# Raw output weights in nine places over the turned cached keys, late stores on ScalarE's queue, and a tile of its own for the sample group's sums

## The chip, the cores and the metric

One core of a Trainium2 chip runs the whole program, one launch. The metric is the device time of that launch in microseconds, the median over the runs shown. A separate profiled execution of the same program gives the trace from which all rows below are taken.

The core has five engines with instruction streams of their own, which meet only at semaphores: TensorE (PE, with its weight loads listed as PEld), VectorE (DVE), ScalarE (ACT), GpSimd (POOL) and SyncE (SP), which here does little but issue DMAs. A DMA is an instruction in the stream of the engine that issues it: if the tile it reads is not ready, or the tile it writes not free, the engine waits there, and everything behind it in that stream waits too. SBUF is the on-chip memory; PSUM holds the sums of matmuls.

## The reference, cut to what matters

One decoder layer over a prompt group (1024 new tokens) and a sample group (8 sequences of 8 tokens with 4096 cached positions). Both go through the same weights:

```python
z = h @ w_in                                  # projections, split into q, k, v, gates ...
o_sb  = stick_breaking(q_a, ..., sb_k, sb_v)  # the sample group's runs over the paged cache cache_sb
o_nsa = nsa_attend(q_b, ...)                  # compressed + selected + window attention
u = concatenate([o_sb * silu(gate_a), o_nsa * silu(gate_b)])
h = x + u @ w_out
y = h + sigmoid(h @ w_ple_gate) * (p @ w_ple)
```

The last two lines, for nine tiles of tokens, are the part of the program that the change is about: `w_out` and `w_ple_gate` are 1024x1024, `w_ple` is 256x1024.

## The kernel before, in words

The program runs in stages: projections for both groups; compression of the cached keys; then, interleaved, the sample group's stick-breaking over the cache (`phase_b`) and the prompt's sparse attention (`nsa_unit` in stage d, one unit for each pair of heads and block `i` of 128 tokens); at last the output projection (`Phase3`). The code states the steps and gives them due times; a scheduling layer then fixes, before the program runs, the order of the instructions in each engine's stream. So a change of a buffer or of a queue can move instructions on all engines.

**The sample group's cache.** Blocks of `cache_sb` arrive by SP's queue in tiles `bkv` (512 KB a load); VectorE turns the keys into `bkT` (L1477); TensorE forms scores `bz` (L1386) and sums `bo` (L1402). `finish` (L1538 to L1545) copies a group's sums into a tile `bs` and stores them to the scratch `s_oa_s` in eight DMAs. It runs twice, `finish(0)` in the middle of the stage and `finish(1)` at its end.

**The prompt's sparse attention.** A unit ends with its sums in PSUM, which ScalarE copies into `u` (printed as line L1731); for the last pair of heads (`pair == 3`) each of the eight units stores its 128x128 block to the scratch `s_uT` by SP's queue (L1278).

**The output projection.** Matmuls run in pieces of fp32r: each weight and each input is split into a high part, which GpSimd rounds off (`woh`, `wgh`, `wph`, L1602; `uh`, L1667), and a low part, which VectorE forms as raw minus high (`wol`, `wgl`, `wpl`, L1603; `ul`, L1668). `weight` takes a weight matrix 128 rows by 512 columns at a time: a raw tile `wr` of 256 KB is loaded by SP's queue (L1601), split, and its place is free again when VectorE is done. `w_out` has 16 such tiles, `w_ple` 4, `w_ple_gate` 16. In the kernel before the raw tiles of `w_out` have two places, in the same pool as `woh`/`wol`; those of the other two weights have three (`nwb`). The pool of `w_out` lies over the end of the cache tiles `bkv`, so it can be filled only once the stick-breaking is nearly over.

`a(t)` forms `h = x + u @ w_out` for a tile `t`: it loads `u`, the gate `g` and `x`, multiplies (L1660 to L1662, with a tanh on ScalarE), splits, and makes 48 products of 128x512 for a prompt tile. The sample group (`t == 8`) needs 32, with high and low part of its 64 tokens side by side in one operand; `product` then adds the two halves, through a tile that it takes from the ring of `g` (one place). `b(t)` is the rest: 48 products with `w_ple_gate`, 12 with `w_ple`. The order is a(8), a(7), a(0), a(6), b(8), b(7), and so on; prompt tiles stand in the order 7, 0, 6, 1, 5, 2, 4, 3. `u`, `g`, `uh` and `ul` have one place each, so `uh` of the next tile can be written only when the products of the tile before have read it.

The figures of the string `P3A` set the number of PSUM sums, of places and the lag; the seventh, `nwr`, is the number of places for the raw tiles of `w_out`.

Of the kernel before, what the change touches and what calls it, by code (L numbers as in the profile page):

```python
# [5 lines left out]
F32 = mybir.dt.float32  # L6
# [14 lines left out]
def hbm(ap, off, dims):  # L21
    return bass.AP(tensor=ap.tensor, offset=ap.offset + off, ap=[list(d) for d in dims])
# [5 lines left out]

def diagonals(K, pool):

    t = pool.tile([128, 128], F32, name="jpf")
    K.nc.gpsimd.iota(t, pattern=[[1, 128]], base=0, channel_multiplier=-1, allow_small_or_imprecise_dtypes=True)
    return t


def make_consts(K, pool):
    nc = K.nc
    K.id = pool.tile([128, 128], F32, name="idf")
    with K.tc.tile_pool(name="cj", bufs=1, reuse_waits="tile") as tmp:
# [899 lines left out]
def phase_d(K, es, part):  # L939
    nc, A, T = K.nc, K.A, K.T  # L940
# [233 lines left out]
    def nsa_unit(pair, h, i, last):  # L1174

        def gen():
# [8 lines left out]
            for c0 in range(0, W, 512):  # L1185
                w = min(512, W - c0)
# [85 lines left out]
            o = slice(i * 128, i * 128 + 128)  # L1272
            if ("u", pair) not in state:
                state["u", pair] = mid.tile([128, 1024], F32, name="u", bufs=1)
            u = state["u", pair]
            K.evac(u[:, o], av[:, :128])
            if pair == 3:
                nc.sync.dma_start(hbm(T["uT"], (512 + pair * 128) * 1024 + i * 128, [[1024, 128], [1, 128]]), u[:, o])  # L1278
            elif last:
                nc.sync.dma_start(hbm(T["uT"], (512 + pair * 128) * 1024, [[1024, 128], [1, 1024]]), u)  # L1280
        return gen
# [4 lines left out]
    if part == "s":  # L1286
# [7 lines left out]
        for pair in range(4):  # L1294
            x = [sb_unit(pair, h, i, i == 3) for i in order for h in range(2)]
# [5 lines left out]
    for pair in range(4):  # L1301
        g = nsa_prep(pair)()
        for t in P["p%d" % pair if pair % 2 == 0 else "p"]:
            L.append((pair * 8 + t, g))
        for n, i in enumerate(order):
            for h in range(2):
                g = nsa_unit(pair, h, i, n == 7)()
# [6 lines left out]
def phase_b(K, es, psb):  # L1314
# [3 lines left out]
    nc, A, T = K.nc, K.A, K.T  # L1318
# [219 lines left out]
    def finish(g4):  # L1538
        assert summed.count(g4) == 128
        o = wk.tile([128, 4, 128], F32, name="bs", bufs=2)  # L1540
        for i in range(4):
            (V.tensor_copy if i % 2 else S_.copy)(o[i * 32:i * 32 + 16], out[g4][i * 32:i * 32 + 16])
        for i in range(4):
            for h2 in range(2):
                nc.sync.dma_start(hbm(T["oa_s"], g4 * 32 * 512 + (i * 2 + h2) * 64, [[512, 8], [8 * 512, 4], [1, 64]]), o[i * 32 + h2 * 8:i * 32 + h2 * 8 + 8, :, h2 * 64:h2 * 64 + 64])  # L1545

    once = lambda f, *x: (f(*x) for _ in range(1))
    P = K.bstep
    g = start()
    L = [(t, g) for t in P["n"]]  # L1550
    for b in range(8):
        g = begin(b)
        L += [(b * 4 + t, g) for t in P["b"]]
        for n in range(4):
            x = Step(b, 3 - n)
# [13 lines left out]
class Phase3:  # L1569
# [3 lines left out]
    def __init__(s, K, es):  # L1573
        s.K = K
        P = lambda n, b, **k: es.enter_context(K.tc.tile_pool(name=n, bufs=b, side="right", **k, reuse_waits="tile"))
        s.wa = P("3a", 1)
        s.ps = [(P("3aps", 1, space=PSUM), K.p3acc[0], 3 - K.p3acc[0])]
        s.h = {}
        s.WO = s.weight(s.wa, "wo", K.A["w_out"], 8, 1)

    def open_b(s, es):
        K = s.K
        P = lambda n, b, **k: es.enter_context(K.tc.tile_pool(name=n, bufs=b, **k, reuse_waits="tile"))
        s.wb = P("3b", 1)
        s.ps.append((P("3bps", 1, space=PSUM), K.p3acc[1], 5 - K.p3acc[1]))
        s.K.nwr = K.nwb
        s.WP = s.weight(s.wb, "wp", K.A["w_ple"], 2, K.wbw)
        s.WG = s.weight(s.wb, "wg", K.A["w_ple_gate"], 8, K.wbw)

    def acc(s):  # L1590
        p, n, _ = s.ps[-1]
        return p.tile([128, 512], F32, name="acc", bufs=n)

    def weight(s, pool, name, src, nk, w):
        nc = s.K.nc
        hi = [pool.tile([128, nk, 512], F32R, name=f"{name}h{n}") for n in range(2)]
        lo = [pool.tile([128, nk, 512], F32R, name=f"{name}l{n}") for n in range(2)]
        for n in range(2):
            for k0 in range(0, nk, w):
                raw = pool.tile([128, w, 512], F32, name="wr", bufs=s.K.nwr if w == 1 else 2)  # L1600
                nc.sync.dma_start(raw, hbm(src, k0 * 128 * 1024 + n * 512, [[1024, 128], [128 * 1024, w], [1, 512]]))  # L1601
                nc.gpsimd.tensor_scalar(hi[n][:, k0:k0 + w], raw, 1.0, 0.0, op0=OP.mult, op1=OP.add)  # L1602
                nc.vector.tensor_tensor(lo[n][:, k0:k0 + w], raw, hi[n][:, k0:k0 + w].bitcast(F32), op=OP.subtract)  # L1603
        return hi, lo

    def product(s, X, W, n, nk, S):

        nc = s.K.nc
        acc = s.acc()
        if not S:  # L1610
            terms = [(a[:, k], b[:, k]) for k in range(nk) for a, b in ((X[0], W[0][n]), (X[0], W[1][n]), (X[1], W[0][n]))]
        else:
            terms = [(X[0][:, k], b[:, k]) for k in range(nk) for b in (W[0][n], W[1][n])]
        for i, (a, b) in enumerate(terms):
            nc.tensor.matmul(acc, a, b, start=i == 0, stop=i == len(terms) - 1)  # L1615
        if not S:
            return acc
        z = s.wa.tile([128, 8, 128], F32, name="g", bufs=1).rearrange("p a b -> p (a b)")[:64, 0:512]
        nc.scalar.copy(z, acc[64:128])
        nc.vector.tensor_tensor(z, acc[:64], z, op=OP.add)  # L1620
        return z
# [133 lines left out]
    return phase_b(K, es, es.enter_context(K.tc.tile_pool(name="psb", bufs=1, space=PSUM, side="right", reuse_waits="tile")))  # L1755


P3A = [int(x) for x in "2,3,3,2,2,1,2,3,1".split(",")]


def stage_d(K, steps, esb):
# [131 lines left out]
```

## Time and profile before

| what | us |
|---|---|
| median of 3 runs | 1827.23 |
| lowest and highest run | 1824.98, 1827.26 |
| the profiled execution | 1825.76 |
| its span in the trace | 1824.0 |

The span runs from the first instruction to the last that the trace shows; the 1.76 us beside it lie around the program. Over the whole span TensorE's matmuls are busy 89% of the time, VectorE 68%, ScalarE 48% and GpSimd 32%. Such shares mix stages with different limits, so the page is only where to begin: the stretch between the attention and the output projection, some 60 us near the end, is read from the timelines, the waits and the chain. The granted clock is the one that the throttle allows TensorE; it shows 1.00 (2.4 GHz) or 0.50 (1.2 GHz), and in a stretch the mean of the two. The mean over the profiled run is 0.946.

### The profile page before, as it was taken

How to read it: one execution, taken by the hardware profiler on the slowest of the kernel's cores; microseconds unless marked ns; L12 is line 12 of the kernel's file. 1: busy time of each engine (PE TensorE's matmuls, PEld its weight loads, DVE VectorE, ACT ScalarE, POOL GpSimd, SP SyncE). 2: the span in 40 equal slices, each digit the busy share in tenths (PEclk: the TensorE clock that was granted, in tenths of full speed). 3: DMA queues.
4: the chain of work that ended last, by engine and by line, in shares of the span. 5: the costliest groups of instructions: out<-in, count | busy, mean ns of one | idle time of the engine just before them, and what ended most of it. 6: DMA issues, size and time to landing. Idle time of an engine off the chain costs nothing.

```text
span 1824.0 us, 41667 instructions
## 1 busy us (share of the span) xinstructions
PE 1618.3 (89%) x15742; PEld 1377.0 (75%) x15742; DVE 1243.9 (68%) x2918; ACT 876.1 (48%) x2200; POOL 591.2 (32%) x1028
## 2 busy tenths in 40 slices
PE   4899999999987799999999679899799798499998
PEld 4799888988865699889888556667567566278887
DVE  5334755876876668888888897877788876645322
ACT  3212645655656334444344367777677777102111
POOL 2123002121311255555553144445244445410000
PEclk9899999999997899999999589999899999699999
DMA  7234113132106365555554997776988782723210
GB/s 252 74 90 126 62 58 117 54 108 63 57 32 147 126 209 193 185 193 198 188 187 142 369 305 251 241 269 224 307 302 289 262 278 67 231 75 93 87 50 35
DMA packets 186899, 300.80 MB, mean 165 GB/s; under 512 B 30145, under 2 KB 100610, under 8 KB 178434
## 3 DMA queue, kind: packets, MB, share of 16 engines
q1 hardware_dynamic: 145786, 207.14, 35.1%
q0 software_dynamic: 9216, 67.11, 11.1%
q10 hardware_dynamic: 31696, 23.88, 4.1%
q8 instruction: 124, 2.03, 0.5%
q14 instruction: 77, 0.63, 0.1%
HBM read 271.81 MB, written 30.48 MB: 166 GB/s over the span
## 4 chain that ended last, share of the span: by engine, by line
PE 39%; DVE 15%; DMA 11%; ACT 6%; issue 4%; POOL 3%; SPq 1%; ACTq 0%; POOLq 0%; DVEq 0%
PE acc L1615 11%; PE H L500 6%; DMA bkv<-in_cache_sb 5%; PE pt L1270 2%; PE bo L1402 2%; DMA raw<-in_cache_nsa,cidx 2%; PE bz L1386 2%; DVE bkT L1477 2%; PE acc L270 2%; PE pt L1247 2%; PE sc L672 2%; ACT bAT L1528 2%; PE cav L814 2%; PE acc L268 1%; DVE bs L1396 1%
## 5 line engine op out<-in xcount | busy, mean ns | idle before, releaser
L270 PE MATMUL acc<-whi,hh 128*128 128x256 f32 (+1 forms) x704 | 204.0, 291 | 5.3 <-DVE og L1733 2.7
L270 PE MATMUL acc<-wlo,hh 128*128 128x256 f32 (+1 forms) x704 | 201.6, 287 | 0.0
L270 PE MATMUL acc<-whi,hl 128*128 128x256 f32 (+1 forms) x704 | 200.7, 290 | 0.0
L1477 DVE STREAM_TRANSPOSE bkT<-bkv 128x512 f32<-128x512 f32 x256 | 171.5, 693 | 41.5 <-DMA bkv<-in_cache_sb 30.6
L270 PEld LDWEIGHTS acc<-whi,hh 128*128 128x128 f32 x704 | 135.1, 192 | 8.1 <-POOL whi L123 3.1
L481 ACT CAST XH<-xt 128x512 fp32r<-128x512 f32 x128 | 79.1, 618 | 122.5 <-PE H L500 112.4
L270 PEld LDWEIGHTS acc<-wlo,hh 128*128 128x128 f32 x704 | 135.1, 192 | 0.2 <-issue 0.2
L270 PEld LDWEIGHTS acc<-whi,hl 128*128 128x128 f32 x704 | 133.3, 192 | 0.7 <-issue 0.3
L1238 POOL TENSOR_SCALAR t<-t,nst 128x640 f32<-128x640 f32 (+7 forms) x128 | 93.4, 731 | 112.0 <-DVE nst L1229 48.4
L123 POOL TENSOR_SCALAR whi<-wraw 128x512 fp32r<-128x512 f32 (+1 forms) x60 | 53.3, 915 | 216.4 <-PE acc L245 153.2
L1247 PE MATMUL pt<-idf,t 128*128 128x128 f32 x528 | 91.7, 291 | 14.1 <-ACT aT L1731 7.0
L1402 PE MATMUL bo<-bkv,bAT 128*16 128x128 f32 x2048 | 84.8, 281 | 19.4 <-POOL bAT L1530 12.2
L651 POOL DMA_INDIRECT raw<-in_cache_nsa,cidx x64 | 66.9, 1046 | 102.5 <-DVE xt L476 53.7
L1386 PE MATMUL bz<-bkT,bQ 128*32 128x128 f32 x2048 | 92.7, 304 | 5.2 <-DVE ba L1506 3.3
L1530 POOL TENSOR_SCALAR bAT<-baT 32x128 f32<-32x128 f32 x256 | 77.6, 303 | 57.8 <-DVE baT L1520 36.8
L1731 ACT COPY aT<-pt 128x512 f32<-128x512 f32 (+3 forms) x167 | 76.9, 475 | 38.0 <-PE pt L1041 20.7
L500 PE MATMUL H<-w1hk,XH 128*128 128x256 f32 (+1 forms) x272 | 86.4, 318 | 9.8 <-ACT XH L481 8.2
L476 DVE STREAM_TRANSPOSE xt<-raw 128x512 f32<-128x512 f32 x132 | 88.0, 679 | 3.1 <-DMA raw<-in_cache_nsa,cidx 1.7
L1247 PEld LDWEIGHTS pt<-idf,t 128*128 128x128 f32 x528 | 59.7, 145 | 39.0 <-issue 13.5
L1085 DVE TENSOR_TENSOR_SCAN t<-ones,t 128x1024 f32<-128x1024 f32 (+7 forms) x64 | 87.0, 1360 | 0.7
L1402 PEld LDWEIGHTS bo<-bkv,bAT 128*16 128x16 f32 x2048 | 58.7, 99 | 36.7 <-POOL bAT L1530 22.3
L486 POOL TENSOR_TENSOR XL<-xt,XH 128x512 fp32r<-128x512 f32 x56 | 72.2, 1289 | 37.8 <-ACT XH L481 37.5
(464 smaller groups left out, 5040.9 us busy)
## 6 DMA issues: line engine op xcount, KB each, us to landing
bkv<-in_cache_sb SPq DMA_DIRECT2D x256, 512.0 KB
wraw<-in_w_in SPq DMA_DIRECT2D x28, 512.0 KB
x<-in_x_prompt SPq DMA_DIRECT2D x8, 512.0 KB
out_sb_rows_prompt<-o ACTq DMA_DIRECT2D x32, 128.0 KB
s_gT<-og ACTq DMA_DIRECT2D x16, 256.0 KB
cwin<-in_state_win SPq DMA_DIRECT2D x8, 512.0 KB
wr<-in_w_out SPq DMA_DIRECT2D x16, 256.0 KB
u<-s_uT SPq DMA_DIRECT2D x8, 512.0 KB
```

The costliest lines, as they stand in the source:

```text
L270: nc.tensor.matmul(acc[:, :w], a[:, k, t * 128:(t + 1) * 128], b[:, k, :w], start=i == 0, stop=i == 23)
L476: V.transpose(xt[:, :, e, :, b], raw[:, :, 0:256].rearrange("p l (k e c) -> p e l k c", e=2, c=32)[:, e])
L481: S_.copy(XH.rearrange("p a b -> p (a b)"), x.rearrange("p e k b s -> p (e k b s)"))
L500: nc.tensor.matmul(H[:m, kv * 256:kv * 256 + 256], x[:, c], y[:, l * 2 + e], start=start and l + kv + e + i == 0, stop=stop and l == 7 and ...
L1085: nc.vector.tensor_tensor_scan(a[:, ::-1], K.ones.to_broadcast([128, W]), a[:, ::-1], 0.0, op0=OP.mult, op1=OP.add)
L1238: nc.gpsimd.tensor_scalar(x, x, c, 1.0, op0=OP.mult, op1=OP.mult)
L1247: nc.tensor.transpose(pt[:, b * 128:(b + 1) * 128], x, K.id)
L1386: nc.tensor.matmul(z(h, g), q(j), kT(j), start=jj == 0, stop=jj == 1, skip_group_check=True, tile_position=(0, h * 32))
L1402: nc.tensor.matmul(oav[i * 32:i * 32 + 16], lhs(g, hp), v[:, i * 128:i * 128 + 128], start=first, stop=last, skip_group_check=True, tile_p ...
L1477: V.transpose(t.kT[f][:, :, i % 4], t.k[i].rearrange("p (j c) -> p j c", j=16))
L1530: G.tensor_scalar(o, i, 1.0, 0.0, op0=OP.mult, op1=OP.add)
L1615: nc.tensor.matmul(acc, a, b, start=i == 0, stop=i == len(terms) - 1)
```

## The change

Three things. First, the raw tiles of `w_out` get a pool of their own, `3r`, with nine places of 2 KB a partition instead of two. It is closed when the weights of `b` are opened. It lies over the place of `bkT`, the turned keys; its first place also overlaps the place of `bs` in `finish(1)`, the second the first bytes of `bkv`, and the other seven overlap only `bkT`. `woh` and `wol` move up by 2 KB a partition and lie over `bkv` as before. The raw tiles of `w_ple` and `w_ple_gate` keep three places. Second, the eight stores of `u` at L1278 and the eight stores of `finish(1)` at L1545 are issued by ScalarE instead of SyncE. Third, the sum of the sample group's two halves gets its own tile `z`, and no longer takes the one place of `g`.

```diff
             if pair == 3:
-                nc.sync.dma_start(hbm(T["uT"], ...), u[:, o])
+                nc.scalar.dma_start(hbm(T["uT"], ...), u[:, o])
...
-                nc.sync.dma_start(hbm(T["oa_s"], ...), o[...])
+                (nc.sync, nc.scalar)[g4].dma_start(hbm(T["oa_s"], ...), o[...])
...
-        s.WO = s.weight(s.wa, "wo", K.A["w_out"], 8, 1)
+        s.raws = ExitStack()
+        s.WO = s.weight(s.wa, "wo", K.A["w_out"], 8, 1, s.raws.enter_context(K.tc.tile_pool(name="3r", bufs=1, side="right", reuse_waits="tile")))
     def open_b(s, es):
         K = s.K
+        s.raws.close()
...
-        s.WP = s.weight(s.wb, "wp", K.A["w_ple"], 2, K.wbw)
-        s.WG = s.weight(s.wb, "wg", K.A["w_ple_gate"], 8, K.wbw)
+        s.WP = s.weight(s.wb, "wp", K.A["w_ple"], 2, K.wbw, s.wb)
+        s.WG = s.weight(s.wb, "wg", K.A["w_ple_gate"], 8, K.wbw, s.wb)
...
-                raw = pool.tile([128, w, 512], F32, name="wr", bufs=s.K.nwr if w == 1 else 2)
+                raw = raws.tile([128, w, 512], F32, name="wr", bufs=s.K.nwr)
...
-        z = s.wa.tile([128, 8, 128], F32, name="g", bufs=1).rearrange("p a b -> p (a b)")[:64, 0:512]
+        z = s.wa.tile([64, 512], F32, name="z", bufs=1)
...
-P3A = [int(x) for x in "2,3,3,2,2,1,2,3,1".split(",")]
+P3A = [int(x) for x in "2,3,3,2,2,1,9,3,1".split(",")]
```

The scheduling layer orders the streams anew. The new lines of the file are two further down (L1601 of before is L1603 after, L1602 is L1604, L1667 is L1669).

SP's stream from the last load of cached keys on, before; `wr` is a raw weight tile, `bs` the sums of `finish(1)`, `hs` and `hq` the residual inputs of the sample group and of the first prompt tile:

```order
L1471 DMA bkv<-in_cache_sb 128x2x512
L1278 DMA s_uT<-u 128x128 x3
L1545 DMA s_oa_s<-bs 8x4x64 x8
L1278 DMA s_uT<-u 128x128
L1601 DMA wr<-in_w_out 128x512 x2
L1652 DMA u<-s_oa_s 64x512
L1653 DMA u<-s_on_s 64x512
L1654 DMA g<-s_g_s 64x1024
L1658 DMA hs<-in_x_sample 64x1024
L1601 DMA wr<-in_w_out 128x512
L1658 DMA hq<-in_x_prompt 128x1024
L1601 DMA wr<-in_w_out 128x512 x2
```

The same place after:

```order
L1471 DMA bkv<-in_cache_sb 128x2x512
L1603 DMA wr<-in_w_out 128x512 x9
L1654 DMA u<-s_oa_s 64x512
L1603 DMA wr<-in_w_out 128x512
L1655 DMA u<-s_on_s 64x512
L1656 DMA g<-s_g_s 64x1024
L1603 DMA wr<-in_w_out 128x512
L1660 DMA hs<-in_x_sample 64x1024
L1603 DMA wr<-in_w_out 128x512 x3
L1660 DMA hq<-in_x_prompt 128x1024
L1603 DMA wr<-in_w_out 128x512 x2
L1659 DMA g<-s_gT 128x8x128
```

All stores are gone from this part of SP's stream; the weight loads stand together, ahead of the sample group's inputs.

GpSimd's stream at the splits of `w_ple_gate` (`wgh`) and of the first prompt tiles (`uh`), before; the last number of a name tells the two halves of a weight apart:

```order
L1602 TENSOR_SCALAR wgh_22182<-wr 128x512 x4
L1602 TENSOR_SCALAR wgh_22183<-wr 128x512 x5
L1667 TENSOR_SCALAR uh<-u 128x1024
L1602 TENSOR_SCALAR wgh_22183<-wr 128x512 x3
L1667 TENSOR_SCALAR uh<-u 128x1024 x7
```

And after:

```order
L1604 TENSOR_SCALAR wph_22167<-wr 128x512 x2
L1669 TENSOR_SCALAR uh<-u 128x1024
L1604 TENSOR_SCALAR wgh_22186<-wr 128x512 x8
L1669 TENSOR_SCALAR uh<-u 128x1024
L1604 TENSOR_SCALAR wgh_22187<-wr 128x512 x8
L1669 TENSOR_SCALAR uh<-u 128x1024 x6
```

Before, 13 of the 16 gate splits stood ahead of the first `uh` and 3 behind it; after, all 16 stand behind the first `uh`, eight ahead of the second and eight ahead of the third.

VectorE's stream at the sample group's second split (`uh<-pt,uh`), before:

```order
L1603 TENSOR_TENSOR wol_21689<-wr,woh_21687 128x512 x2
L1637 TENSOR_TENSOR uh<-pt,uh 128x4x64 x2
L1603 TENSOR_TENSOR wol_21689<-wr,woh_21687 128x512 x3
L1603 TENSOR_TENSOR wol_21690<-wr,woh_21688 128x512
L1620 TENSOR_TENSOR g<-acc,g 64x512
```

And after:

```order
L1605 TENSOR_TENSOR wol_21692<-wr,woh_21690 128x512 x3
L1605 TENSOR_TENSOR wol_21693<-wr,woh_21691 128x512
L1664 SCALAR_TENSOR_TENSOR u<-g,u 64x1024
L1605 TENSOR_TENSOR wol_21693<-wr,woh_21691 128x512 x7
L1639 TENSOR_TENSOR uh<-pt,uh 128x4x64 x2
```

Before, the sample group's input was split in the middle of the low parts of `w_out`; after, it stands behind the last of all 16.

## Rows read from the trace of the kernel before

**Rows 1.** The page, its head and part 1: the span, then each engine with busy time, share of the span and instructions.

```profile
span 1824.0 us, 41667 instructions
PE 1618.3 (89%) x15742; PEld 1377.0 (75%) x15742; DVE 1243.9 (68%) x2918; ACT 876.1 (48%) x2200; POOL 591.2 (32%) x1028
```

**Rows 2.** Busy time by stretches of the span: the stretch, busy us of PE, PEld, DVE, ACT and POOL (with the count of instructions), then the granted clock of TensorE as a share of full speed, the mean busy share of the DMA engines, and GB/s. The stretches overlap where one lies inside another.

```profile
1540.00:1560.00 20.00, 16.54 (x127) 12.08 (x127) 9.57 (x15) 7.55 (x17) 10.26 (x14) 0.83 0.62 177
1558.60:1598.00 39.40, 14.79 (x36) 6.25 (x32) 26.71 (x35) 3.50 (x7) 20.15 (x28) 0.57 0.75 237
1570.00:1578.00 8.00, 3.81 (x10) 1.68 (x10) 4.03 (x7) 0.64 (x2) 3.94 (x6) 0.50 1.00 369
1598.00:1601.60 3.60, 3.53 (x8) 2.33 (x9) 2.69 (x3) 0.00 (x0) 1.34 (x3) 0.50 0.92 291
1612.00:1623.50 11.50, 11.32 (x48) 8.85 (x48) 4.27 (x4) 1.06 (x1) 0.06 (x1) 1.00 0.17 48
1620.00:1820.00 200.00, 196.81 (x899) 161.31 (x897) 69.74 (x95) 30.04 (x51) 6.35 (x6) 1.00 0.19 60
```

**Rows 3.** All instructions that touch the raw weight tile wr: count, duration in ns (min/median/max), first and last start in us; then who waited for it (us, times).

```profile
L1601 SPq DMA_DIRECT2D wr<-in_w_out x16: 327/328/361, 1535.7 to 1578.3; - x16
L1602 POOL TENSOR_SCALAR woh<-wr x16: 616/621/1123, 1538.9 to 1581.5; 128x512 fp32r<-128x512 f32 x16
L1603 DVE TENSOR_TENSOR wol<-wr,woh x16: 679/693/1097, 1539.6 to 1582.6; 128x512 fp32r<-128x512 f32 x16
L1602 POOL TENSOR_SCALAR wgh<-wr x16: 620/774/1166, 1575.2 to 1602.1; 128x512 fp32r<-128x512 f32 x16
...
  PEld acc L1615: 17.4, 18
```

**Rows 4.** Timeline of SyncE's queue, 1500 to 1625 us: start and length in us, line, out<-in, how many in the row. A row of several takes in the waits between them.

```profile
1503.09 25.05 SPq L1278 DMA_DIRECT2D s_uT<-u  x3
1530.23 3.91 SPq L1545 DMA_DIRECT2D s_oa_s<-bs  x8
1535.28 0.35 SPq L1278 DMA_DIRECT2D s_uT<-u  x1
1535.75 1.10 SPq L1601 DMA_DIRECT2D wr<-in_w_out  x2
...
1578.30 0.33 SPq L1601 DMA_DIRECT2D wr<-in_w_out  x1
...
1587.40 0.38 SPq L1657 DMA_DIRECT2D g<-s_gT  x1
```

**Rows 5.** Waits of SyncE's queue, 1480 to 1640 us: what waited, for what, us in total, times, longest.

```profile
SPq L1278 <- ACT u L1731: 34.3, 6, 16.8
...
SPq L1601 <- DVE wol L1603: 11.7, 11, 1.8
```

**Rows 6.** The chain that ended last, pieces in order of time: start, us, what.

```profile
1532.81 0.71 DVE bs L1542
...
1536.52 2.42 DMA wr<-in_w_out
...
1611.02 1.06 POOL uh L1667
...
1623.59 1.06 POOL uh L1667
1624.69 19.48 PE acc L1615 x84
```

**Rows 7.** Timeline of TensorE: start, us, line, operation, shapes, and in brackets the idle time before it and what ended it.

```profile
1558.54 0.48 PE L1270 MATMUL pt<-aW,vc 128*64 128x128 f32 x3
...
1583.78 0.80 PE L1615 MATMUL acc<-wol,uh 128*128 128x512 f32 x1 [0.76 <-DVE wol L1603]
...
1598.06 0.79 PE L1615 MATMUL acc<-woh,uh 128*128 128x512 f32 x1 [9.26 <-POOL uh L1667]
```

**Rows 8.** Timeline of VectorE, the same columns.

```profile
1582.62 1.10 DVE L1603 TENSOR_TENSOR wol<-wr,woh 128x512 fp32r<-128x512 f32 x1
...
1586.70 0.68 DVE L1671 SCALAR_TENSOR_TENSOR hs<-g,hs 64x512 f32<-64x512 f32 x1
...
1592.08 1.23 DVE L1660 TENSOR_TENSOR u<-u,g 128x1024 f32<-128x1024 f32 x1 [0.34 <-DMA g<-s_gT]
...
1594.87 1.62 DVE L1662 SCALAR_TENSOR_TENSOR u<-g,u 128x1024 f32<-128x1024 f32 x1
```

**Rows 9.** Timeline of GpSimd, the same columns.

```profile
1541.91 1.23 POOL L1238 TENSOR_SCALAR t<-t,nst 128x512 f32<-128x512 f32 x1
...
1543.39 0.69 POOL L1238 TENSOR_SCALAR t<-t,nst 128x512 f32<-128x512 f32 x1
...
1596.65 1.36 POOL L1667 TENSOR_SCALAR uh<-u 128x1024 fp32r<-128x1024 f32 x1 [1.22 <-DVE u L1662]
```

**Rows 10.** Issues of stores, ns min/median/max: by ScalarE's queue elsewhere in the program (L276), and those of both finish steps by SyncE's (L1545).

```profile
L276 ACTq DMA_DIRECT2D s_gT<-og x16: 326/327/542, 219.1 to 556.1; - x16
...
L1545 SPq DMA_DIRECT2D s_oa_s<-bs x16: 264/289/1057, 1285.5 to 1533.9; - x16
```

**Rows 11.** Timeline of ScalarE in the last part of the prompt's sparse attention, and the tanh of tile 7's gate.

```profile
1534.06 0.81 ACT L1226 ACTIVATE t<-t,nst 128x640 f32<-128x640 f32 x1
...
1593.34 1.06 ACT L1661 ACTIVATE g<-g 128x1024 f32<-128x1024 f32 x1 [4.75 <-DVE u L1660]
```

More of the change, by code (lines that the diff above doesn't have):

```diff
@@ L1277, in gen @@
             if pair == 3:
-                nc.sync.dma_start(hbm(T["uT"], (512 + pair * 128) * 1024 + i * 128, [[1024, 128], [1, 128]]), u[:, o])
+                nc.scalar.dma_start(hbm(T["uT"], (512 + pair * 128) * 1024 + i * 128, [[1024, 128], [1, 128]]), u[:, o])
             elif last:
@@ L1544, in finish @@
             for h2 in range(2):
-                nc.sync.dma_start(hbm(T["oa_s"], g4 * 32 * 512 + (i * 2 + h2) * 64, [[512, 8], [8 * 512, 4], [1, 64]]), o[i * 32 + h2 * 8:i * 32 + h2 * 8 + 8, :, h2 * 64:h2 * 64 + 64])
+                (nc.sync, nc.scalar)[g4].dma_start(hbm(T["oa_s"], g4 * 32 * 512 + (i * 2 + h2) * 64, [[512, 8], [8 * 512, 4], [1, 64]]), o[i * 32 + h2 * 8:i * 32 + h2 * 8 + 8, :, h2 * 64:h2 * 64 + 64])
     once = lambda f, *x: (f(*x) for _ in range(1))
@@ L1592, in acc, with weight @@
         return p.tile([128, 512], F32, name="acc", bufs=n)
-    def weight(s, pool, name, src, nk, w):
+    def weight(s, pool, name, src, nk, w, raws):
         nc = s.K.nc
```

## The prediction

> **What bounds the kernel now.** I read the page's head and part 1 first [rows 1]: TensorE's matmuls are busy 89% of the span, so what can be won is where TensorE stands still. The table by stretches shows where: from 1558.6 to 1598 us it is busy 14.79 us of 39.4, at a mean granted clock of 0.57; from 1620 to 1820 it is busy 196.81 us of 200 at clock 1.00 [rows 2]. Behind 1620 us little can be won; what the change brings must come from those 39.4 us.
>
> The timeline of TensorE says what stands in the gap: the last product of the sparse attention starts at 1558.54, the last of the sample group's 32 products at 1583.78, released by a low part `wol`, and the first product of a(7) at 1598.06, after 9.26 us of waiting for GpSimd's `uh` [rows 7]. So there are two delays in a row: the weights, then the inputs of tile 7.
>
> The weights: 16 raw tiles are issued from 1535.7 to 1578.3, 42.6 us, and the splits follow them [rows 3]. A split costs 0.621 us on GpSimd and 0.693 on VectorE [rows 3]; it is the two places that stretch them, since each load waits until VectorE has freed a place (11.7 us in 11 waits) and in order behind other loads [rows 5].
>
> The inputs of tile 7: the sample group's sum takes the place of `g`, so SP can load the gate of tile 7 (1587.40, [rows 4]) only when VectorE has added that sum into `hs` at 1586.70 [rows 8]. From there VectorE multiplies at 1592.08 and 1594.87, GpSimd splits at 1596.65 [rows 8, 9].
>
> **Part 1: the first load.** SP's stream loses the stores, which stood ahead of the weights: three stores of `u` with their waits took 25.05 us, the eight of `bs` 3.91 [rows 4], and in the longer stretch the waits of these stores for ScalarE's copies come to 34.3 us [rows 5]. But the first place of the new pool overlaps `bs`, so the first weight load must now wait until the eight stores have read it and landed. ScalarE is to issue them; its queue pays 0.327 us an issue elsewhere [rows 10], SP paid 0.289 [rows 10]. VectorE's last copy of `bs` ends at 1533.52 [rows 6]; six of the stores come behind it at 0.3: 1535.3; about 2.2 us to land (a 256 KB load takes 2.42, [rows 6]; a store of 8 KB isn't in a row, so 1 to 2.5): 1537.5. The first load was at 1535.75 [rows 4], so this part costs 1.8 us (0.5 to 4 with the bounds). The late stores win nothing here: the first weight waits for the same `bs`.
>
> The Trainium skill (DMA: Bandwidth & Descriptors, section "Issuing engines are not separate DMA queues") says that DMAs of all issuing engines run on the same 16 DMA engines, and that spreading them over issuers saves only the time to issue them. By that rule the move is worth at most 16 issues; the wait of 34.3 us, which is order and not data, would be no gain either, and the sum below counts none.
>
> ScalarE pays for the stores: six in a row stand ahead of its softmax work for the last units, which is late in the attention's chain (its exponential at 1534.06 takes 0.81, [rows 11]): 6 x 0.3 = 1.8 us, and a wait for VectorE's copy of 1.3. The attention's last products then come at about 1561, not 1558.5. What hides that is the splitting of the weights, which is later still; without this cover it would cost 2 to 3 us.
>
> **Part 2: the weights.** Nine loads go in a row, 2.36 MB; at 237 to 369 GB/s [rows 2] that is 6.4 to 10 us. The other seven each find a place freed by then. So the splits set the pace. Run side by side the two engines slow each other: GpSimd's scaling of 128x512 takes 1.23 us beside a `wol` and 0.69 alone [rows 9], and the splits reach 1.12 and 1.10 [rows 3]. I take 1.1 us a split, near the slow end, as both engines now run without gaps: 17.6 us for 16, and 5 us for the attention's own work on these engines in between. First raw there at 1540.0, last `wol` done at 1563 (at 0.7 each 1556, at 1.3 each, which is one engine after the other, 1566). Before, it ended at 1583.72 [rows 8]: 20 us earlier.
>
> In VectorE's stream the sample group's second split now stands behind all 16 `wol`, so the 32 products no longer trickle along with the weights but run in one piece from about 1564.5. TensorE has been idle, so the first run at half clock: the first eight products of a(7) took 3.53 us at granted clock 0.50 (1.2 GHz), then 48 took 11.32 at 1.00 (2.4 GHz) [rows 2]. Eight at 0.44 and 24 at 0.236 are 9.2 us (7.6 all fast, 14.1 all slow): a(8) ends at 1573.7.
>
> **Part 3: the inputs of tile 7.** With `z` apart, the gate's load waits for the sample's first product only, not for its last sum. Its work (1.23 and 1.62 on VectorE, 1.06 for the tanh, 1.36 for `uh`, [rows 8, 9, 11]) is 5.3 us behind the splits, so done around 1571, hidden under a(8). I put the first product of a(7) at 1577, a little behind a(8) for `uh` and the transposes between: 21 us earlier than 1598.06. If the load of `u` lands late, as below, it is 1580 to 1585.
>
> **Part 4: what is given back.** GpSimd's stream now has eight gate splits between `uh` of tile 7 and of tile 0, and eight more ahead of tile 6; before, 13 of the 16 were done ahead of the first `uh`, in TensorE's idle time. They keep three places. Their rate before: 16 from 1575.2 to 1602.1 [rows 3], 26.9 us / 15 = 1.79 us each. Eight are 14.3, and `uh` is 1.06 [rows 6]: a tile each 16 us with the gaps, where before a(7) to a(6) took 1624.69 - 1598.06 = 26.6 us for two [rows 6, 7], most of it products. So a(6) starts at 1577 + 32 = 1609, 15.7 us earlier than 1624.69. With 1.3 us a split (three of each eight are loaded ahead) the cycle would be back at TensorE's own 13 us and 21 are kept; with 2.4 us it is 20 us, and 8 are kept.
>
> TensorE idles about 4 us in each cycle, and after idle stretches the granted clock was 0.50: eight products at half clock cost 3.53 - 8 x 0.236 = 1.6 us. Twice, and a little for the transposes: 3.3 us. Behind a(6) the streams are nearly those of before, with 3.2 us lost in 200 [rows 2]; but ScalarE now has a fourth gate's tanh ahead of the sample group's last sums, and I take as much again, 3.2 (0 to 4).
>
> **The sum**, against the profiled execution: 1825.76 - 15.7 + 3.3 + 3.2 = 1816.6. The median of the runs shown is 1.47 us over it: 1818.0.
>
> **The rivals.**
>
> *Nothing is given back.* The gate splits are loaded ahead while a(8) and a(7) run and keep 1.3 us, the clock stays at 1.00. For it: three places full when GpSimd comes to them. Against: VectorE's last gate splits of each half now stand behind the addition of a(7)'s own sums. Gain 21 - 3.2 or 15.7 with no clock loss, 15 to 18: 1810 to 1812.
>
> *The transfers are the bound.* Up to the load of tile 7's `u`, SP now issues 16 x 0.262 + 2 x 0.262 of `w_ple` and 2.4 MB of inputs, about 7.1 MB; at 237 GB/s that is 30 us (1568, harmless), at the 177 GB/s of 1540 to 1560 [rows 2] it is 40 us: 1578, a(7) at 1585, 13 earlier, of which 5 more are given back and 6.5 go as above: a gain of 1 to 3, 1824 to 1826. For it: the DMA engines were busy a share of 1.00 at 1570 to 1578 [rows 2].
>
> *Slower: the gate splits pace the tiles.* Two tiles now hang on 16 splits. a(6) starts at 1577 + 2 x 1.06 + 16 s; it is as late as before from s = 2.84 us a split, and with the clock's 3.3 from 2.63. Loads that compete with `u`, `g` and `hp` of three tiles could do that; at 2.9 us the end is 1825.8 + 1 + 3.3 + 1.5: 1831.6. Against: 1.79 was measured with the same three places and with DMA near full.
>
> *It doesn't do what it says:* the first load waits for ScalarE's whole stream, say 10 us, as that engine was the attention's own pace. Then the weights come 8 us later and about 8 are lost of 9.5: 1826. I count it with the transfers.
>
> **How the numbers follow.** Forecast, 1814 to 1822: 0.58. Nothing given back, 1808 to 1813: 0.16. Transfers or late stores, 1822 to 1827: 0.19. Slower: 0.07. The range leaves out the slower case and the outer part of the gain: 1810.5 to 1826. A measurement of this kernel can tell 0.2%, 3.65 us, from no change: faster means below 1823.6. All of the first two cases and a third of the third are there: 0.80. Same 0.13, slower 0.07.
>
> **What would show it.** Right: the first load of `w_out` near 1537.5; nine in a row; the last `wol` at 1560 to 1566; the sample group's products in one run; the first product of a(7) at 1575 to 1579 with no wait for `hs`; then TensorE waiting for `uh` of tiles 0 and 6 some 4 us each, with GpSimd busy on `wgh` ahead of them and a granted clock below 1.00 between 1580 and 1615. Wrong: a first load behind 1541, splits over 1.3 us each, `u` of tile 7 landing behind 1575, or gate splits off 1.79 by half a microsecond, which alone is worth 8 us of the sum.

## The result, and the profile after

The changed kernel took 1812.83 us in the median of 13 runs (1801.89 to 1823.43), beside 1825.92 of 13 runs of the kernel before; the ratio is 0.9939, 95% interval 0.9924 to 0.9954. By the ratio that is 11.1 us off 1825.92; the two medians lie 13.1 us apart. The forecast was 1818.0, 9.2 us off the 1827.23 that was known then, with a range of 1810.5 to 1826.

The head of the page and its first part for the changed kernel, against [rows 1]:

```profile
span 1813.7 us, 41664 instructions
...
PE 1617.2 (89%) x15742; PEld 1380.4 (76%) x15742; DVE 1244.2 (69%) x2918; ACT 874.7 (48%) x2200; POOL 598.1 (33%) x1028
```

The span is 10.3 us shorter and TensorE's busy time the same within 1.1 us, so nearly all of the gain is time in which TensorE stood still.

Busy time by stretches: busy us of PE, PEld, DVE, ACT and POOL, the granted clock, the DMA share, GB/s. The last two rows are parts of the stretch behind a(6):

```profile
1540.00:1560.00 20.00, 10.85 (x85) 9.17 (x87) 13.90 (x25) 8.98 (x21) 18.47 (x22) 0.72 0.96 273
1560.00:1580.00 20.00, 14.56 (x78) 10.90 (x74) 14.55 (x19) 3.88 (x8) 10.55 (x11) 0.84 0.82 255
1580.00:1600.00 20.00, 18.36 (x77) 14.01 (x77) 16.23 (x20) 1.43 (x2) 10.75 (x11) 0.93 0.68 212
1600.00:1620.00 20.00, 16.82 (x67) 13.18 (x66) 12.97 (x13) 3.23 (x4) 4.95 (x6) 0.91 0.36 109
1629.45:1639.45 10.00, 8.02 (x30) 5.99 (x29) 7.16 (x11) 4.19 (x7) 0.00 (x0) 0.83 0.36 103
1609.45:1813.70 204.25, 196.48 (x882) 160.71 (x882) 68.24 (x94) 30.11 (x51) 5.27 (x5) 0.98 0.19 59
```

Between 1580 and 1600 TensorE is busy 18.36 us of 20; in [rows 2] the stretch from 1558.6 to 1598 had 14.79 of 39.4. But from a(6) on this kernel takes 204.25 us to the end, where the one before took 1824.0 - 1624.69 = 199.3. The row from 1629.45 shows 2 us of that, at a clock of 0.83. The ten us right behind a(6), which had waited 3.19 us for `uh`, were granted 0.83 too: 37 matmuls in them, 45 in the next ten.

The raw weight tiles, against [rows 3]:

```profile
L1603 SPq DMA_DIRECT2D wr<-in_w_out x16: 327/406/433, 1538.3 to 1556.0; - x16
L1604 POOL TENSOR_SCALAR woh<-wr x16: 611/616/2963, 1542.3 to 1562.9; 128x512 fp32r<-128x512 f32 x16
L1605 DVE TENSOR_TENSOR wol<-wr,woh x16: 673/1086/1171, 1543.0 to 1564.4; 128x512 fp32r<-128x512 f32 x16
L1604 POOL TENSOR_SCALAR wgh<-wr x16: 613/947/2478, 1577.7 to 1607.8; 128x512 fp32r<-128x512 f32 x16
```

The loads of `w_out` now span 17.7 us instead of 42.6, and the last `wol` starts at 1564.4 instead of 1582.6. The median `wol` takes 1.086 us instead of 0.693, beside splits that now follow each other closely on GpSimd; GpSimd's own median stays at 0.616, with single splits up to 2.963. VectorE has one long gap in this stretch: the product of the sample group's `u` stands among the `wol` and waits for the gate `g`, whose load now comes behind ten weight loads on SyncE:

```profile
1553.38 1.34 DVE L1662 TENSOR_TENSOR u<-u,g 64x1024 f32<-64x1024 f32 x1 [4.05 <-DMA g<-s_g_s]
```

SyncE's queue, against [rows 4]: nine loads in a row, and the gate of tile 7 (L1659) loaded before the sample group's last sum, not behind it.

```profile
1538.35 4.14 SPq L1603 DMA_DIRECT2D wr<-in_w_out  x9
...
1558.70 0.38 SPq L1659 DMA_DIRECT2D g<-s_gT  x1
...
1566.65 0.38 SPq L1658 DMA_DIRECT2D u<-s_uT  x1
```

TensorE, against [rows 7]: the last sum `bo` of the stick-breaking, the first of the 32 products of a(8), and the first products of a(7), a(0) and a(6).

```profile
1530.17 1.93 PE L1402 MATMUL bo<-bkv,bAT 128*16 128x128 f32 x62
...
1566.55 0.79 PE L1617 MATMUL acc<-woh,uh 128*128 128x512 f32 x1
...
1577.81 0.50 PE L1617 MATMUL acc<-woh,uh 128*128 128x512 f32 x1 [1.67 <-POOL uh L1669]
...
1593.39 0.50 PE L1617 MATMUL acc<-woh,uh 128*128 128x512 f32 x1 [0.89 <-POOL uh L1669]
...
1609.45 0.50 PE L1617 MATMUL acc<-woh,uh 128*128 128x512 f32 x1 [3.19 <-POOL uh L1669]
```

VectorE at the end of the weights:

```profile
1562.42 3.12 DVE L1605 TENSOR_TENSOR wol<-wr,woh 128x512 fp32r<-128x512 f32 x3 [0.52 <-POOL woh L1604]
1565.46 0.41 DVE L1639 TENSOR_TENSOR uh<-pt,uh 128x256 fp32r<-128x256 f32 x1
1567.06 0.42 DVE L1639 TENSOR_TENSOR uh<-pt,uh 128x256 fp32r<-128x256 f32 x1 [1.19 <-ACT uh L1638]
...
1574.87 0.68 DVE L1673 SCALAR_TENSOR_TENSOR hs<-z,hs 64x512 f32<-64x512 f32 x1
...
1581.07 1.09 DVE L1673 SCALAR_TENSOR_TENSOR hs<-z,hs 64x512 f32<-64x512 f32 x1
```

The sample group's input is split at 1565.46, behind the last `wol`, and its sums reach `hs` at 1574.87 and 1581.07. The first product of tile 7 waits for neither; its third, at 1579.23, waits 0.69 us for the second `z`.

GpSimd between the weights and the tiles:

```profile
1571.32 1.04 POOL L1604 TENSOR_SCALAR wph<-wr 128x512 fp32r<-128x512 f32 x1 [5.30 <-DMA wr<-in_w_ple]
1576.12 0.62 POOL L1604 TENSOR_SCALAR wph<-wr 128x512 fp32r<-128x512 f32 x1 [3.76 <-DMA wr<-in_w_ple]
1576.71 1.04 POOL L1669 TENSOR_SCALAR uh<-u 128x1024 fp32r<-128x1024 f32 x1
...
1592.29 1.04 POOL L1669 TENSOR_SCALAR uh<-u 128x1024 fp32r<-128x1024 f32 x1
...
1608.36 1.04 POOL L1669 TENSOR_SCALAR uh<-u 128x1024 fp32r<-128x1024 f32 x1
```

`uh` of tile 7 stands behind four splits of `w_ple`, two of which wait 5.30 and 3.76 us for their loads. But it takes the one place of the sample group's `uh`, which a(8) reads until 1575.31, so these waits cost it at most 1.4 us.

Behind it the gate splits wait for their loads, and the loads wait for places that VectorE frees (what waited, for what, us, times, longest):

```profile
POOL wgh L1604 <- DMA wr<-in_w_ple_gate: 12.8, 9, 3.2
```
```profile
SPq L1603 <- DVE wgl L1605: 13.5, 13, 2.3
```

Spans of single executions differ by what happens long before this part: in the profiles of this study the last `bo` ends anywhere from 1523.7 to 1534.1, also between kernels whose edits differ only behind it (e4 and e7). So the table counts, in each profile, from the end of that `bo` (1529.58 before, 1532.10 after). All in us; the ratio is that of the timed runs to the kernel before, with its interval. The times of each row come from one profile; kernels whose streams are alike up to a(7) agree there within 1 us (e4 and e7; e8 and e10; e9, e11 and e12).

| kernel | first `w_out` load | last `wol` starts | a(7) | a(6) | end | ratio |
|---|---|---|---|---|---|---|
| before | 6.2 | 53.0 | 68.5 | 95.1 | 294.4 | 1 |
| changed | 6.2 | 32.3 | 45.7 | 77.4 | 281.6 | 0.9939 (0.9924 to 0.9954) |
| e1, stores alone | 3.2 | 50.3 | 65.0 | 96.7 | 296.0 | 1.0019 (1.0002 to 1.0036) |
| e2, stores back | 6.7 | 32.8 | 47.8 | 78.7 | 283.2 | 0.9925 (0.9903 to 0.9948) |
| e3, no `z` | 3.0 | 32.1 | 58.3 | 93.7 | 293.0 | 1.0008 (0.9988 to 1.0028) |
| e4, `z`, two places | 6.2 | 48.2 | 50.9 | 78.7 | 280.4 | 0.9913 (0.9889 to 0.9938) |
| e5, gate loads left out | 6.2 | 33.1 | 46.5 | 83.3 | 286.1 | 0.9971 (0.9955 to 0.9986) |
| e6, four gate places | 6.2 | 34.3 | 48.3 | 78.7 | 280.1 | 0.9943 (0.9920 to 0.9966) |
| e7, e4 + four gate places | 6.2 | 47.8 | 50.5 | 79.4 | 281.3 | 0.9946 (0.9926 to 0.9967) |
| e8, eight places | 3.0 | 31.7 | 40.3 | 73.1 | 277.4 | 0.9907 (0.9880 to 0.9934) |
| e9, six places | 3.0 | 32.0 | 41.7 | 70.5 | 277.2 | 0.9925 (0.9898 to 0.9952) |
| e10, e8 + later b(8) | 3.0 | 31.7 | 40.3 | 72.9 | 274.2 | 0.9917 (0.9890 to 0.9944) |
| e11, e9 + later b(8) | 3.0 | 31.7 | 41.1 | 70.6 | 274.8 | 0.9900 (0.9871 to 0.9929) |
| e12, e11 + four gate places | 3.0 | 32.2 | 41.9 | 71.9 | 274.9 | 0.9891 (0.9864 to 0.9917) |

### The profile page after: what moved, and what is told of

Its sections match the earlier page's. It is cut to its first block, busy times and chain, and to the rows that moved or that the text cites. A ratio compares the mean times of both kernels' runs of the same rounds, so it can differ in the third digit from the quotient of the medians.

```text
span 1813.7 us, 41664 instructions
## 1 busy us (share of the span) xinstructions
PE 1617.2 (89%) x15742; PEld 1380.4 (76%) x15742; DVE 1244.2 (69%) x2918; ACT 874.7 (48%) x2200; POOL 598.1 (33%) x1028
## 3 DMA queue, kind: packets, MB, share of 16 engines
q0 software_dynamic: 9216, 67.11, 11.1%
## 4 chain that ended last, share of the span: by engine, by line
PE 38%; DVE 14%; DMA 11%; ACT 6%; issue 4%; POOL 3%; SPq 1%; ACTq 0%; POOLq 0%; DVEq 0%
PE acc L1617 10%; PE H L500 5%; DMA bkv<-in_cache_sb 4%; DMA raw<-in_cache_nsa,cidx 3%; PE bo L1402 2%; PE bz L1386 2%; PE pt L1270 2%; DVE bkT L1477 2%; PE pt L1247 2%; PE acc L270 2%; ACT bAT L1528 2%; PE sc L672 2%; PE cav L814 1%; PE acc L268 1%; PE z L1201 1%
## 5 line engine op out<-in xcount | busy, mean ns | idle before, releaser
L1402 PE MATMUL bo<-bkv,bAT 128*16 128x128 f32 x2048 | 90.6, 297 | 21.3 <-POOL bAT L1530 13.7
L1530 POOL TENSOR_SCALAR bAT<-baT 32x128 f32<-32x128 f32 x256 | 77.2, 302 | 57.8 <-DVE baT L1520 36.8
L1402 PEld LDWEIGHTS bo<-bkv,bAT 128*16 128x16 f32 x2048 | 62.4, 104 | 40.4 <-POOL bAT L1530 21.6
```

The lines of the kernel that those rows point to most:

```text
L1402: nc.tensor.matmul(oav[i * 32:i * 32 + 16], lhs(g, hp), v[:, i * 128:i * 128 + 128], start=first, stop=last, skip_group_check=True, tile_p ...
L1530: G.tensor_scalar(o, i, 1.0, 0.0, op0=OP.mult, op1=OP.add)
```

## The experiments

**e1: the stores alone.** The kernel before, and of the change only this:

```diff
-                nc.sync.dma_start(hbm(T["uT"], ...), u[:, o])
+                nc.scalar.dma_start(hbm(T["uT"], ...), u[:, o])
...
-                nc.sync.dma_start(hbm(T["oa_s"], ...), o[...])
+                (nc.sync, nc.scalar)[g4].dma_start(hbm(T["oa_s"], ...), o[...])
```

> The kernel before with the sixteen late stores on ScalarE's queue and nothing else; two places for the raw w_out tiles, the sum in the place of g. Theory (nine places and the own tile z bring the gain, the stores nothing): within 3 us of before. Rival S (SyncE's queue, freed of stores, brings it): 8 to 11 us faster than before.

Measured: ratio 1.0019, no gain; by the ratio it is 3.5 us slower, just past the 3 us that were expected. The first load does come 3.0 us earlier, since two places do not overlap `bs` and it no longer stands behind the stores; the last `wol` is 2.7 us earlier and a(7) 3.5, and a(6) is 1.6 later. Rival S is out.

**e2: the stores back on SyncE**, all else as changed:

```diff
-                nc.scalar.dma_start(hbm(T["uT"], ...), u[:, o])
+                nc.sync.dma_start(hbm(T["uT"], ...), u[:, o])
...
-                (nc.sync, nc.scalar)[g4].dma_start(hbm(T["oa_s"], ...), o[...])
+                nc.sync.dma_start(hbm(T["oa_s"], ...), o[...])
```

> The changed kernel with all sixteen late stores back on SyncE's queue; nine places and z stay. Theory: 9 to 13 us faster than before, as the changed kernel, since the first weight waits for the tile bs in either case. Rival S: less than 4 us faster than before.

Measured: 0.9925, the gain of the changed kernel without the stores' move. By both runs it is worth nothing that can be told. What it costs ScalarE shows as a wait in the changed kernel, where six of the stores take its stream from 1534.04 to 1537.06, the last of them behind VectorE's copy of `bs`, which ends at 1536.39 (what waited, for what, us, times, longest):

```profile
ACT u L1733 <- DMA s_oa_s<-bs: 2.5, 1, 2.5
```

**e3: no own tile `z`**, all else as changed:

```diff
-        z = s.wa.tile([64, 512], F32, name="z", bufs=1)
+        z = s.wa.tile([128, 8, 128], F32, name="g", bufs=1).rearrange("p a b -> p (a b)")[:64, 0:512]
```

> The changed kernel with the sample group's sum back in the one place of g; nine places and the stores on ScalarE stay. Theory: the gate of tile 7 waits again for the last sum, hs at about 1582; a(7) starts some 11 us behind that, near 1593, but more gate splits are done ahead of it: 2 to 6 us faster than before. Rival Z (the own tile alone brings the gain): within 2 us of before. Rival S: 8 to 11 us faster.

Measured: 1.0008, nothing left of the gain, though the weights end as early as in the changed kernel. The last sum into `hs` on VectorE, the gate's load on SyncE and the first product of a(7) on TensorE:

```profile
1581.79 0.67 DVE L1673 SCALAR_TENSOR_TENSOR hs<-g,hs 64x512 f32<-64x512 f32 x1
```
```profile
1582.49 0.38 SPq L1659 DMA_DIRECT2D g<-s_gT  x1
```
```profile
1592.43 0.80 PE L1617 MATMUL acc<-woh,uh 128*128 128x512 f32 x1 [9.03 <-POOL uh L1669]
```

The load is issued 0.03 us behind that sum's end, and a(7) starts 10.6 us behind its start; in the kernel before it was 11.4 (1586.70 to 1598.06, [rows 7, 8]). I had put a(7) at 1593 and was right in that, but had expected 2 to 6 us of gain to be left; rival Z holds. By the table a(7) is 10.2 us earlier than before, a(6) only 1.4. The rest went between the two, which take 35.3 us here against 26.6 before: nine gate splits stand between the first and the second `uh` instead of three, and from a(7) to a(6) the splits wait 12.4 us for their loads.

**e4: the own tile `z`, without the nine places and the stores' move**: two places in the new pool, stores on SyncE; the changed kernel with the stores' lines as in e2, and:

```diff
-P3A = [int(x) for x in "2,3,3,2,2,1,9,3,1".split(",")]
+P3A = [int(x) for x in "2,3,3,2,2,1,2,3,1".split(",")]
```

> The own tile z alone: the raw w_out tiles have two places (in the pool of their own), the stores are on SyncE's queue. Theory: the weights still end near 1580, a(7) starts near 1585 instead of 1598, and the splits of the other two weights all come behind it: 2 to 7 us faster than before. Rival Z: 9 to 12 us faster.

Measured: 0.9913, all of the gain: 14.0 us by the table, 12.8 for the changed kernel. My theory (2 to 7) falls; rival Z holds and its 9 to 12 are passed (15.9 by the ratio). The low parts of `w_out`, and TensorE at the end of a(8), at a(7) and at a(6):

```profile
L1605 DVE TENSOR_TENSOR wol<-wr,woh x16: 677/692/1093, 1540.4 to 1578.7; 128x512 fp32r<-128x512 f32 x16
```
```profile
1578.69 0.80 PE L1617 MATMUL acc<-woh,uh 128*128 128x512 f32 x1 [0.73 <-POOL woh L1604]
...
1581.40 0.80 PE L1617 MATMUL acc<-woh,uh 128*128 128x512 f32 x1 [1.18 <-POOL uh L1669]
...
1609.20 0.50 PE L1617 MATMUL acc<-woh,uh 128*128 128x512 f32 x1 [0.58 <-POOL uh L1669]
```

The weights end 16 us later than in the changed kernel, but most products of a(8) have run along with them, and a(7) starts 2.7 us behind the last pair. In the changed kernel it is 13.4 us between the last `wol` and a(7). So 16 us of earlier weights, with the stores moved, bring a(7) 5.2 us forward, a(6) 1.3 and the end nothing. The pair that differs in the places alone is e2 and e4, both with `z` and with the stores on SyncE: there nine places bring a(7) 3.1 us forward, a(6) nothing, and the end is 2.8 later.

e4 is not the kernel before with `z` and nothing else: its raw tiles lie in the pool of their own, and its last `wol` starts 4.8 us earlier than before. No run has `z` without that pool, so what the pool adds is not shown.

**e5: gate loads left out.** The changed kernel, with only three of the 16 tiles of `w_ple_gate` loaded; the gate in y is made of those three:

```diff
+                if name == "wg" and (n or k0 >= 3):
+                    raw = old[(n * 8 + k0) % 3]
+                else:
...
```

> The changed kernel, but 13 of the 16 raw tiles of w_ple_gate aren't loaded: their splits read the first three again, so the part of y with the gate is computed from wrong weights. Every split still runs. Theory G (with nine places the gate splits wait for their loads and hold back uh of tiles 0 and 6): a(6) starts at 1602 to 1605 instead of 1609.45, 15 to 19 us faster than before. Rival (the splits' own time on GpSimd and VectorE, or the clock, holds the tiles): 9 to 13 us faster, as the changed kernel.

Measured: 0.9971, 5.3 us faster than before, less than the theory and its rival both had. The scheduling layer put all 16 gate splits ahead of the second `uh`, GpSimd's rows:

```profile
1575.99 18.42 POOL L1609 TENSOR_SCALAR wgh<-wr 128x512 fp32r<-128x512 f32 x16
1598.07 1.04 POOL L1674 TENSOR_SCALAR uh<-u 128x1024 fp32r<-128x1024 f32 x1 [3.66 <-DVE u L1669]
```

Without a load to wait for, the 16 splits take 18.42 us, 1.15 each; in the changed kernel the first and the last start 30.1 us apart, 2.0 each. So there the loads do pace them. But here `uh` of tile 0 stands behind all 16 and waits another 3.66 for VectorE, which has the low parts ahead of its product, and a(7) to a(6) grew to 36.8 us. Since the order changed along with the loads, the run does not price the loads alone.

**e6: four places for the gate weights**, all else as changed:

```diff
-P3A = [int(x) for x in "2,3,3,2,2,1,9,3,1".split(",")]
+P3A = [int(x) for x in "2,3,3,2,2,1,9,4,1".split(",")]
```

> The changed kernel with four places instead of three for the raw tiles of w_ple and w_ple_gate. Theory G: eight splits take some 12 us instead of 15, a(6) starts near 1605, 13 to 16 us faster than before. Rival: 9 to 13 us faster.

Measured: 0.9943, as the changed kernel, 10.4 us faster than before, as the rival had it. The fourth place does speed the splits: the first and the last start 26.1 us apart instead of 30.1, and they wait 10.4 us for loads instead of 12.8. But the order moved as well: eleven of them stand ahead of `uh` of tile 0 instead of eight. a(7) to a(6) takes 30.4 us, 1.2 less, where theory G had 4, and `uh` of tile 6 now waits for TensorE itself:

```profile
1609.94 1.04 POOL L1669 TENSOR_SCALAR uh<-u 128x1024 fp32r<-128x1024 f32 x1 [3.97 <-PE acc L1617]
```

**e7: e4 with four gate places** (`"2,3,3,2,2,1,2,4,1"`).

> The kernel of e4 (own tile z, two places for w_out, stores on SyncE) with four places instead of three for the gate weights. Theory G: a(0) and a(6) there follow at TensorE's own pace already (14.8 and 13.0 us), so a fourth place brings 1 to 2 us more than e4: 15 to 18 us faster than before. Rival (two places bind the gain, not the gate splits): as e4, 14 to 16.

Measured: 0.9946, no better than e4, and by the ratio, some 10 us, below both ranges. The splits are faster here too (first and last start 24.1 us apart, 32.2 in e4), but four of them instead of two stand ahead of `uh` of tile 0 and nine instead of seven between it and that of tile 6. a(7) to a(6) takes 28.8 us, 1.0 more.

**e8: eight places for `w_out`** (`"2,3,3,2,2,1,8,3,1"`), all else as changed. No place overlaps `bs`.

> The changed kernel with eight places for w_out, none of which overlaps bs, so the first load need not wait for the stores of finish(1) to land. Theory G: the first load is issued some 4 us earlier, and that is given back at the gate splits: 9 to 13 us faster than before, as the changed kernel. Rival L (the late first load costs the nine places their worth): 14 to 17 us faster.

Measured: 0.9907; by the table 4.2 us less than the changed kernel. The first load on SyncE, the first split of the sample group's input on VectorE, then the first product of a(8), a(7) and a(6) on TensorE:

```profile
1530.76 7.07 SPq L1603 DMA_DIRECT2D wr<-in_w_out  x8
```
```profile
1556.42 0.41 DVE L1639 TENSOR_TENSOR uh<-pt,uh 128x256 fp32r<-128x256 f32 x1
```
```profile
1558.12 0.50 PE L1617 MATMUL acc<-woh,uh 128*128 128x512 f32 x1
...
1568.11 0.79 PE L1617 MATMUL acc<-woh,uh 128*128 128x512 f32 x1 [2.44 <-POOL uh L1669]
...
1600.90 0.50 PE L1617 MATMUL acc<-woh,uh 128*128 128x512 f32 x1 [3.21 <-POOL uh L1669]
```

The first load is 3.2 us earlier, but the last `wol` only 0.6. What moved is the order: VectorE splits the sample group's input after 12 of the 16 low parts, so a(8) starts 30.3 us behind the last `bo` and not 34.5, and `uh` of tile 7 stands ahead of the last split of `w_ple`. So rival L has the size, and the earlier load is at most a part of the reason. The intervals of the timed runs of e8 and of the changed kernel overlap, so the 4.2 us rest on one profile of each.

**e9: six places** (`"2,3,3,2,2,1,6,3,1"`), chosen as its streams go further in this: the sample group's split after ten low parts, `uh` of tile 7 ahead of all of `w_ple`, `uh` of tile 0 ahead of all gate splits.

> The changed kernel with six places for the raw w_out tiles. In its streams VectorE splits the sample group's input after the tenth low part of w_out instead of the sixteenth, and GpSimd forms uh of tile 7 ahead of w_ple, uh of tile 0 ahead of the gate splits. Theory O (what counts is where the small inputs stand among the splits, not how early the weights end): counted from the last product bo of the stick-breaking, a(7) starts at 40 us or earlier (45.7 with nine), a(6) at 66 to 71 (77.4), 16 to 21 us faster than before. Rival W (the pace of the weights counts, and fewer places are slower): last wol later than 32.3, a(7) as with two places at 48 to 51, 12 to 15 us faster than before.

Measured: 0.9925; by the table the end is as in e8. The low parts of `w_out`, and a(7) and a(6):

```profile
L1605 DVE TENSOR_TENSOR wol<-wr,woh x16: 674/1091/1172, 1542.3 to 1563.4; 128x512 fp32r<-128x512 f32 x16
```
```profile
1573.10 0.50 PE L1617 MATMUL acc<-woh,uh 128*128 128x512 f32 x1 [0.16 <-POOL uh L1669]
...
1601.96 0.50 PE L1617 MATMUL acc<-woh,uh 128*128 128x512 f32 x1 [1.86 <-POOL uh L1669]
```

Three places fewer, and the last `wol` starts 32.0 us behind `bo`, as with nine: the mechanism of rival W is out, six places keep the splits as busy as nine. a(7) is at 41.7, a little past the 40 of theory O, and a(6) at 70.5, within its 66 to 71. The end is not as theory O had it: by the ratio the gain is 13.7 us, under its 16 to 21.

**e10: e8 with b(8) one tile later** (`"2,3,3,2,3,1,8,3,1"`).

> The kernel of e8 (eight places) with b of the sample group one tile later in the program. Theory T (the 5 us that the changed kernel loses behind a(6) come from the sample group's sums z, which stand on VectorE behind the product of the next tile's u): two of them and the half clock behind them go, 2 to 4 us faster than e8 from a(6) to the end, 19 to 22 us faster than before. Rival: the stall only moves, as e8, 15 to 18.

Measured: 0.9917 in the timed runs, whose interval holds e8 and the changed kernel too; by the table 3.2 us less than e8, nearly all behind a(6). By the ratio the gain is 15.1 us, as the rival had it and not the theory. For the theory's stall in the changed kernel, the chain that ended last:

```profile
1628.20 3.88 DMA u<-s_uT
1632.18 1.22 DVE u L1662
1633.40 0.61 DVE z L1622
1634.14 1.19 PE acc L1617 x2
```

The load of the next `u`, VectorE's product of it and only then the sum `z`, for which TensorE waits; its next products run at half clock. In e10 the sums of b(8) stand a tile later, in the stretch from 1640 to 1660:

```profile
1640.00:1660.00 20.00, 18.37 (x87) 14.70 (x87) 9.10 (x13) 6.77 (x11) 0.00 (x0) 1.00 0.28 79
```

1.6 us are still lost, 1.26 and 0.37 of them in waits for `z` (1.60 at the longest in the changed kernel), but at clock 1.00. So the half of theory T on the clock holds; the wait itself moved and hardly shrank. About half of the 3.2 us lies ahead of it: the first ten us behind a(6) hold 43 matmuls at clock 1.00 here and 36 at 0.83 in e8. Why the clock differs there is not shown.

**e11: e9 with b(8) one tile later** (`"2,3,3,2,3,1,6,3,1"`).

> The kernel of e9 with b of the sample group one tile later. Theories O and T together: 18 to 24 us faster than before. If W or the rival of T holds: 12 to 18.

Measured: 0.9900, some 18 us faster than before; by the table 2.4 less than e9.

**e12: e11 with four gate places** (`"2,3,3,2,3,1,6,4,1"`).

> The kernel of e11 with four places for the raw tiles of w_ple and w_ple_gate. uh of tile 0 stands ahead of all gate splits, nine of them ahead of uh of tile 6. If the places of the gate weights still pace the splits, a(6) starts 1 to 3 us earlier than in e11 (70.6 behind the last bo): 19 to 24 us faster than before. If the splits' own time and their place in the stream set it: as e11, 16 to 20.

Measured: 0.9891. a(6) is at 71.9, not earlier than in e11. The fourth place speeds the splits again (first and last start 23.4 us apart instead of 31.2, with 10.4 us of waits for loads instead of 19.0), but nine of them instead of seven stand ahead of `uh` of tile 6. So the tiles hang on the place of `uh` among the splits, as in e6 and e7. e11 and e12 are the fastest timed here, about 1% under the kernel before; between the two nothing can be told.

## Why the prediction was right in its number and wrong in one of its reasons

**The total** was right: 9.2 us forecast, 11.1 measured (13.1 between the medians), in the range, and most of the times on the way there held in the profile: first load at 1538.35 (forecast 1537.5), last `wol` done at 1565.5 (1563), a(8) in one run of 8.8 us from 1566.55 (9.2), a(7) at 1577.81 (1577), a(6) at 1609.45 (1609). That these times match so closely is in part luck: in this profile the last `bo` ends 2.5 us later than in the one before. Counted from it, a(7) came 22.8 us forward where 21 were forecast, and a(6) 17.7 where it was 15.7.

**Part 1, the stores:** right. "The late stores win nothing here": e1 and e2. The rule of the Trainium skill that was weighed (DMA: Bandwidth & Descriptors, section "Issuing engines are not separate DMA queues") agrees with this measurement: 1.0019 with the stores moved alone. The first load waits for `bs` as said; counted from the last `bo` it is at 6.2 before and after, so the cost of 1.8 against before was not there: the load was issued 1.3 us behind the last store's issue, and 2.2 had been put down for landing. Without the overlap it is at 3.0.

**Part 2, the weights: the step that failed.** It read two delays one after the other, the weights and then the inputs of tile 7, and took the first at its full length: in the rival on the late stores, weights 8 us later lose about 8. The time of the weights was right: on GpSimd the 16 splits took 16.2 us and the attention's work between them 4.7, where 17.6 and 5 had been put down. The worth was not. e4 has `z` without the early weights, which end 16 us later there, and gains all. e3 has the early weights without `z`, and gains nothing at the end. The second delay hung on the shared place of `g`, and with that wait gone weights that end nearly as late as before let a(7) start at 50.9 instead of 68.5. Of the 22.8 us by which a(7) came forward, 17.6 come with `z` and the new pool (e4) and 5.2 more with the places and the stores; taken in the other order, 10.2 come with the places and the stores (e3) and 12.6 more with `z`. So no fixed share of a(7) belongs to either; at the end, `z` is needed and the nine places are not. What ate the places' 16 us is in the changed kernel's own rows: a(8) as one run behind the last split, 8.8 us, in place of products along with the weights, and up to 1.4 us for splits of `w_ple` that wait for loads ahead of `uh` of tile 7. The prediction had the first as a fact (the 32 products "in one piece") without counting it against the places.

**Part 3, `z`:** the mechanism was right: the gate of tile 7 is loaded before the sample group's sum. The sum gives `z` no share of its own; that it was held far too small shows in e4's expectation (2 to 7 us).

**Part 4, what is given back:** a(7) to a(6) took 31.6 us (forecast 32), and for the reason given. Behind `uh` of tile 7 eight gate splits take 14.6 us and the next `uh` 1.04 (14.3 and 1.06 forecast); the splits wait 12.8 us for their loads, and the loads 13.5 us for places. A fourth place made the row of 16 splits 4 to 8 us shorter in e6, e7 and e12. What the expectations of e6 and e7 missed is that this hardly brings the tiles forward (1.2 us in e6, nothing in e7 and e12): more splits then stand ahead of the `uh`. With `uh` of tile 0 ahead of all of them a(7) to a(6) takes 28.9 us (e9). TensorE waited 0.89 and 3.19 us for `uh` of tiles 0 and 6, less than the 4 each that were forecast.

The loss behind a(6) was 4.9 us, forecast 3.2 and a part of the clock's 3.3. It was put to ScalarE's tanh; the chain shows VectorE's product of the next `u`, and the rows show a clock of 0.83 behind that wait and behind a(6)'s own. Moving b(8) gave back 2.4 to 3.2 us by the profiles (e10, e11).

**The rivals.** By its number the median, 1812.83, lies in the band of the first rival, nothing given back (1808 to 1813), and 1.2 us below the forecast's own band of 1814 to 1822. The rival's mechanism is not what the trace shows: the gate splits took 2.0 us each and not 1.3, and the clock was 0.93 and 0.91 from 1580 to 1620. The other three did not come true. The one that mattered was not among them: that one of the three edits, with the new pool beside it, is enough for all of the gain.

What stays open: how much of e8's and e9's 4 us is the earlier first load and how much the order, since the scheduling layer moves both at once; what the new pool adds to `z`; and what the gate loads cost by themselves.

## What to carry to other kernels

Where two waits stand one behind the other in a gap, ask for each what is left of it if the other is unchanged: here an own tile of 2 KB a partition, in place of a shared one, was worth 14 us by the profile (with the raw weights in the new pool), and weights 16 us earlier nothing on top of it. More places make an order, not only a supply: a fourth place made the gate splits faster and the tiles no earlier. Look in the new streams for what was woven in before and now stands behind the whole block. And in a program whose start of a stage wanders by several us from run to run, count from an event at that stage's start before comparing profiles.

## What was not expected of the hardware

The forecast's 1.1 us a split held on the whole, the median `wol` being 1.086 us. But single scalings of 128x512 on GpSimd took up to 2.963 us, against 0.616 in the median and 0.611 at the least in the same row; no run shows why. The last `bo` ends some 7 us apart in profiles of kernels whose edits differ only behind it (1530.46 in e4, 1523.73 in e7), so one span is no measure of an edit of a few us here.
